# A softmax over 16,384 rows with held stores, growing tiles and a row-maximum step on GpSimd

## The chip, the cores and the metric

The kernel runs on one core of a Trainium2 chip. The metric is the device time of one execution, in microseconds (us). The profile covers the span from the first to the last instruction of one of these executions. On this core four engines matter: VectorE (DVE), ScalarE (ACT), GpSimd (POOL) and SyncE (SP). Sixteen DMA engines move data between the large memory (HBM) and the on-chip memory (SBUF). Each instruction stream that issues transfers feeds a queue of its own on all sixteen of them.

## The reference

The input is 16 x 1024 rows of 512 single-precision numbers. Each row gets a softmax with temperature 2:

```python
x_scaled = x / 2.0
x_max = np.max(x_scaled, axis=-1, keepdims=True)
exp_x = np.exp(x_scaled - x_max)
return exp_x / np.sum(exp_x, axis=-1, keepdims=True)
```

Input and output are 33.55 MB each. A softmax doesn't change when the same number is subtracted from all elements of a row, so the number that is subtracted is a choice within what the exponential can represent.

## The kernel before

Rows are counted here per partition: the 16,384 rows are 128 for each of the 128 partitions, and "a row" below means one row on every partition, 262,144 bytes.

`PLAN` (L11 to L14) lists twelve tiles. A tile is what one load and one store move. Each entry has the tile's chunks, in rows, and the place where the tile begins in the arena, a buffer of 100 rows in SBUF. A chunk is what one step of VectorE and ScalarE treats. There are tiles of 3, 7, seven times 15, and then 7, 3 and 3 rows. The result replaces the input in the same place of the arena. The first eight tiles have places of their own; the last four reuse the places of earlier tiles, and `behind` (L63 to L68) lists whose. Each partition's part of a tile is one contiguous run, 2,048 bytes per row of the tile, so a transfer is 128 runs, eight on each DMA engine.

Per chunk k there are four steps:

- `do_max` (L83): VectorE reduces each row to its negated maximum in `negmax`, once the tile's load has landed.
- `compute_and_store`, L109 to L121: ScalarE computes the exponential of 0.5 times the input plus `negmax`, row by row, in place, and sums each row into `sums`. The shift is the whole maximum, not half of it.
- `do_mul` (L92): VectorE takes the reciprocal of the sums and multiplies each row by it.
- L131 to L141: SP waits for the last multiply of a tile and issues its store.

VectorE's order is written out at L124 to L128: the maximum of chunk k, then the multiplies of chunk k - LAG, with LAG of 2. So it treats the maximum of two later chunks before it needs a chunk's sums.

Loads of the first eight tiles are issued by ScalarE at the beginning, two of them ahead of the program's opening barrier (`issue_loads`, L77). Loads of the last four are issued by SP, on the same queue as the stores, two stores after the store whose place they take and after waits on that store's landing (L135 to L139). At the end SP waits for every store (L140 to L141). Each tile has a semaphore for its load and one for its store, and s_max, s_exp, s_rec and s_mul count chunks through the four steps.

Of the kernel before, what the change touches and what calls it, by code (L numbers as in the profile page):

```python
# [1 line left out]

# [4 lines left out]

PLAN = [  # L11
    ([3], 0), ([4, 3], 3), ([5] * 3, 10), ([5] * 3, 25), ([5] * 3, 40), ([5] * 3, 55),
    ([5] * 3, 70), ([5] * 3, 85), ([5] * 3, 10), ([4, 3], 3), ([3], 0), ([3], 25),
]  # L14
ARENA = 100
LAG = 2


@with_exitstack
def kernel(  # L20
    ctx: ExitStack,
    tc: tile.TileContext,
    x: bass.AP,
    out: bass.AP,
):
    nc = tc.nc
    fp32 = mybir.dt.float32

    xf = x.flatten_outer_dims()
    of = out.flatten_outer_dims()  # L30
    N, D = xf.shape
    P = nc.NUM_PARTITIONS
    n_rows = N // P
    assert sum(sum(c) for c, _ in PLAN) == n_rows

    arena = nc.alloc_sbuf_tensor("arena", (P, ARENA, D), fp32)
    negmax = nc.alloc_sbuf_tensor("negmax", (P, n_rows), fp32)
    sums = nc.alloc_sbuf_tensor("sums", (P, n_rows), fp32)
    recip = nc.alloc_sbuf_tensor("recip", (P, n_rows), fp32)

    tiles, chunks, base = [], [], 0
    for t, (cs, at) in enumerate(PLAN):
        r = sum(cs)
        tiles.append((base, r, at))
        o = 0
        for c in cs:
            chunks.append((t, base + o, c, at + o))
            o += c  # L50
        base += r
    last_chunk = {c[0]: k for k, c in enumerate(chunks)}

    def dram(ap, t):
        b, r, _ = tiles[t]
        return ap[b * P : (b + r) * P].rearrange("(p r) d -> p r d", r=r)

    def sb(t):
        _, r, at = tiles[t]
        return arena[:, at : at + r, :]  # L60


    behind = {}  # L63
    for t, (_, r, at) in enumerate(tiles):
        for u in range(t):
            _, ru, au = tiles[u]
            if at < au + ru and au < at + r:
                behind.setdefault(t, []).append(u)  # L68

    ld = [tc.alloc_semaphore(f"ld{t}") for t in range(len(tiles))]  # L70
    st = [tc.alloc_semaphore(f"st{t}") for t in range(len(tiles))]
    s_max = tc.alloc_semaphore("s_max")
    s_exp = tc.alloc_semaphore("s_exp")
    s_rec = tc.alloc_semaphore("s_rec")
    s_mul = tc.alloc_semaphore("s_mul")

    def issue_loads(begin, end):  # L77

        for t in range(begin, end):
            if t not in behind:  # L80
                nc.scalar.dma_start(out=sb(t), in_=dram(xf, t)).then_inc(ld[t], 16)

    def do_max(k):  # L83
        t, b, c, a = chunks[k]
        nc.vector.reduce_max(  # L85
            out=negmax[:, b : b + c],
            in_=arena[:, a : a + c],
            axis=mybir.AxisListType.X,
            negate=True,
        )._wait_ge(ld[t], 16).then_inc(s_max, 1)  # L90

    def do_mul(k):  # L92
        t, b, c, a = chunks[k]
        nc.vector.reciprocal(  # L94
            out=recip[:, b : b + c], in_=sums[:, b : b + c]
        )._wait_ge(s_exp, k + 1).then_inc(s_rec, 1)
        for r in range(c):
            ins = nc.vector.tensor_scalar_mul(  # L98
                out=arena[:, a + r],
                in0=arena[:, a + r],  # L100
                scalar1=recip[:, b + r : b + r + 1],
            )
            if r == 0:
                ins._wait_ge(s_rec, k + 1)
        ins.then_inc(s_mul, 1)

    def compute_and_store():

        for k, (t, b, c, a) in enumerate(chunks):  # L109
            for r in range(c):  # L110
                ins = nc.scalar.activation(  # L111
                    out=arena[:, a + r],
                    in_=arena[:, a + r],
                    func=mybir.ActivationFunctionType.Exp,
                    bias=negmax[:, b + r : b + r + 1],
                    scale=0.5,
                    accum_out=sums[:, b + r : b + r + 1],
                )
                if r == 0:
                    ins._wait_ge(s_max, k + 1)  # L120
            ins.then_inc(s_exp, 1)  # L121


        for k in range(len(chunks) + LAG):  # L124
            if k < len(chunks):
                do_max(k)
            if k >= LAG:
                do_mul(k - LAG)  # L128


        late = sorted(behind)  # L131
        for t in range(len(tiles)):
            nc.sync.wait_ge(s_mul, last_chunk[t] + 1)
            nc.sync.dma_start(out=dram(of, t), in_=sb(t)).then_inc(st[t], 16)
            while late and max(behind[late[0]]) <= t - 2:  # L135
                u = late.pop(0)
                for v in behind[u]:
                    nc.sync.wait_ge(st[v], 16)
                nc.sync.dma_start(out=sb(u), in_=dram(xf, u)).then_inc(ld[u], 16)  # L139
        for t in range(len(tiles)):  # L140
            nc.sync.wait_ge(st[t], 16)  # L141

    hook = nc.inst_callbacks[-1]
    nc.remove_inst_callback(hook)
    symbolic = nc._always_lower_symbolic_ap
    nc._always_lower_symbolic_ap = False
    here = str(nc.cur_bb)
    entry = nc.main_func.blocks[0]  # L150
    head, jumps = entry.instructions[:-5], entry.instructions[-5:]
    entry.instructions = []
    nc.switch_bb("main", None)
    issue_loads(0, 2)
    first = list(entry.instructions)
    at = next(k for k, i in enumerate(head) if type(i).__name__ == "InstDrain")
    entry.instructions = head[:at] + first + head[at:]
    issue_loads(2, len(tiles))
    compute_and_store()
    entry.instructions = list(entry.instructions) + jumps  # L160
    nc.switch_bb(here, None)
    nc._always_lower_symbolic_ap = symbolic
    nc.push_inst_callback(hook)


# [1 line left out]
_INS = ['x']  # L167
_OUTS = [((16, 1024, 512), 'float32')]


# [23 lines left out]
```

## Time and profile before

| what | value |
|---|---|
| median of four executions | 162.87 us (162.7 to 163.48) |
| the profiled execution | 163.48 us |
| its span | 161.7 us |
| bytes read / written | 33.55 MB / 33.55 MB |
| mean transfer rate over the span | 415 GB/s |
| maximum of a 5-row chunk (DVE) | 2,814 ns, 21 of them |
| multiply of one row (DVE) | 482 ns, 128 of them, one begun every 0.41 us |
| exponential of one row (ACT) | 710 ns, 128 of them, one begun every 0.70 us |
| small set-up fill on GpSimd | 99 to 102 ns, 4 of them |

The profile's page begins with the busy time of each engine as a share of the span. Its second part cuts the span into 40 equal slices, one digit each: 9 means busy for 90% or more. The row called DMA there is the mean over the sixteen DMA engines. A third part has the DMA queues: q10 is ScalarE's, q1 is SP's; the figures are packets, megabytes, and the time the packets took as a share of sixteen engines' span. The chain of waits is followed back from the last instruction to what released it, and so on to the beginning; it doesn't always follow transfers. An instruction's duration includes its start and its drain, and the next of its engine can begin before it ends, so the distance from start to start is what a series costs.

### The profile page before, as it was taken

The page shows a single profiled execution, that of the slowest core. Times are in us where ns is not written, and L with a number is a line of the kernel's source. Part 1 is how long each engine was busy: PE and PEld are TensorE (multiplying, and loading weights), DVE is VectorE, ACT ScalarE, POOL GpSimd, SP SyncE. Part 2 cuts the span into 40 slices and gives each one's busy share as a digit, 9 for nine tenths or more (in the row PEclk, how much of TensorE's full clock was granted, in tenths as well). Part 3 has the DMA queues.
Part 4 walks back from the last instruction along what each step waited for, and adds up shares of the span by engine and source line. Part 5 has one row for each costly group of instructions (what it writes and reads, how often), then busy time and mean ns, then how long its engine had stood idle before and what let it go on. Part 6 is the DMA issues. An engine that isn't in the chain of part 4 may idle for free.

```text
span 161.7 us, 513 instructions
## 1 busy us (share of the span) xinstructions
DVE 126.3 (78%) x184; ACT 94.5 (58%) x257; POOL 0.2 (0%) x4
## 2 busy tenths in 40 slices
DVE  0475599999999999998899839999999999930000
ACT  0739087866688666787378625667976875500000
POOL 0000000000000000000000000000000000000000
DMA  7999999899999999999999899999999999999991
GB/s 275 450 410 456 418 436 438 340 472 394 463 395 458 395 464 403 448 426 433 456 403 471 388 458 403 456 388 420 448 391 465 441 426 441 448 418 433 396 409 76
DMA packets 3460, 67.14 MB, mean 415 GB/s; under 512 B 385, under 2 KB 385, under 8 KB 1153
## 3 DMA queue, kind: packets, MB, share of 16 engines
q1 hardware_dynamic: 2304, 40.90, 59.1%
q10 hardware_dynamic: 1152, 26.21, 38.5%
q14 instruction: 4, 0.02, 0.0%
HBM read 33.55 MB, written 33.55 MB: 415 GB/s over the span
## 4 chain that ended last, share of the span: by engine, by line
DVE 74%; DMA 10%; another core or an unknown queue 3%; issue 0%; DVEq 0%
DVE negmax L85 40%; DVE arena L98 32%; DMA arena<-in_x_dram 10%; DVE recip L94 2%; DVEq L189 0%
## 5 line engine op out<-in xcount | busy, mean ns | idle before, releaser
L111 ACT ACTIVATE arena<-arena,negmax 128x512 f32<-128x512 f32 x128 | 90.7, 710 | 42.0 <-DVE negmax L85 42.0
L85 DVE TENSOR_REDUCE negmax<-arena 128x5 f32<-128x2560 f32 (+2 forms) x28 | 72.3, 2585 | 15.8 <-DMA arena<-in_x_dram 15.8
L98 DVE TENSOR_SCALAR arena<-arena,recip 128x512 f32<-128x512 f32 x128 | 53.2, 482 | 1.0
L111 ACT ACTIVATION_READ_ACCUMULATOR arena<-arena,negmax 128x1 f32 x128 | 23.9, 187 | 0.0
L94 DVE RECIPROCAL recip<-sums 128x5 f32<-128x5 f32 (+2 forms) x28 | 4.9, 176 | 0.0
L111 ACT ACT_TABLE_LOAD x1 | 1.3, 1283 | 4.5 <-issue 4.5
L178 POOL MEMSET const-bfloat16-1.0<- 128x1 bf16 x1 | 0.1, 102 | 0.0
L178 POOL MEMSET const-uint8-127<- 128x1 uint8 x1 | 0.1, 102 | 0.0
L178 POOL MEMSET const-float32-0.0<- 128x1 f32 x1 | 0.1, 99 | 0.2 <-issue 0.2
L178 POOL MEMSET const-float32-1.0<- 128x1 f32 x1 | 0.1, 99 | 0.0
## 6 DMA issues: line engine op xcount, KB each, us to landing
out_dram<-arena SPq DMA_DIRECT2D x7, 3840.0 KB, 26.0
arena<-in_x_dram ACTq DMA_DIRECT2D x6, 3840.0 KB, 48.1
arena<-in_x_dram SPq DMA_DIRECT2D x1, 3840.0 KB, 36.0
out_dram<-arena SPq DMA_DIRECT2D x2, 1792.0 KB, 17.0
out_dram<-arena SPq DMA_DIRECT2D x3, 768.0 KB, 17.1
arena<-in_x_dram ACTq DMA_DIRECT2D x1, 1792.0 KB, 8.4
arena<-in_x_dram SPq DMA_DIRECT2D x1, 1792.0 KB, 39.8
arena<-in_x_dram SPq DMA_DIRECT2D x2, 768.0 KB, 39.7
```

What stands on the lines that cost most here:

```text
L85: nc.vector.reduce_max(out=negmax[:, b : b + c], in_=arena[:, a : a + c], axis=mybir.AxisListType.X, negate=True,)._wait_ge(ld[t], 16).the ...
L94: nc.vector.reciprocal(out=recip[:, b : b + c], in_=sums[:, b : b + c])._wait_ge(s_exp, k + 1).then_inc(s_rec, 1)
L98: ins = nc.vector.tensor_scalar_mul(out=arena[:, a + r], in0=arena[:, a + r], scalar1=recip[:, b + r : b + r + 1],)
L111: ins = nc.scalar.activation(out=arena[:, a + r], in_=arena[:, a + r], func=mybir.ActivationFunctionType.Exp, bias=negmax[:, b + r : b + r ...
L178: nc = _bacc.Bacc("TRN2", target_bir_lowering=False, num_devices=1)
```

## The change

The plan has ten tiles instead of twelve, with rows 3, 5, 9, 15, 21, 21, 21, 15, 11, 7. The first seven have places of their own in the arena (96 of its 100 rows), the last three reuse places. Chunks have up to 7 rows.

Stores are held: no store is issued before chunk `HOLD` (4) has been multiplied. From then on a store follows its tile's last multiply as before.

Late loads move from SP's queue to ScalarE's. ScalarE issues the load of tile 7 after the exponentials of the last chunk of tile 4, and those of tiles 8 and 9 after the last chunk of tile 5 (`AFTER`), each behind waits for the stores whose places they take.

Between the maximum and the exponential there is a new step: GpSimd multiplies the chunk's negated maxima by 0.5 into a new small tensor `bias`, and ScalarE's exponential takes `bias` and waits for that step's semaphore instead of the maximum's. The shift is then half the maximum, as in the reference.

The closing waits for stores are on GpSimd instead of SP, and stores that nobody else waits for share one semaphore.

```diff
 PLAN = [
-    ([3], 0), ([4, 3], 3), ([5] * 3, 10), ([5] * 3, 25), ([5] * 3, 40), ([5] * 3, 55),
-    ([5] * 3, 70), ([5] * 3, 85), ([5] * 3, 10), ([4, 3], 3), ([3], 0), ([3], 25),
+    ([3], 0), ([5], 3), ([5, 4], 8), ([5] * 3, 17), ([7] * 3, 33), ([7] * 3, 54),
+    ([7] * 3, 75), ([5] * 3, 0), ([6, 5], 15), ([4, 3], 26),
 ]
 ARENA = 100
 LAG = 2
+HOLD = 4
+AFTER = {7: 4, 8: 5, 9: 5}
+EARLY = 2
+FIRST = [("scalar", [(0, 128)])]
...
+    bias = nc.alloc_sbuf_tensor("bias", (P, n_rows), fp32)
...
-    def issue_loads(begin, end):
-
-        for t in range(begin, end):
-            if t not in behind:
-                nc.scalar.dma_start(out=sb(t), in_=dram(xf, t)).then_inc(ld[t], 16)
+    def do_load(engine, t, groups=((0, P),)):
+        for u in behind.get(t, []):
+            engine.wait_ge(st[u], 16)
+        for p, q in groups:
+            engine.dma_start(out=sb(t)[p:q], in_=dram(xf, t)[p:q]).then_inc(ld[t], 16)
+
+    def do_early():
+        for name, groups in FIRST:
+            do_load(getattr(nc, name), 0, groups)
+        for t in range(1, EARLY):
+            do_load(nc.scalar, t)
...
+        for t in range(EARLY, len(tiles)):
+            if t not in behind:
+                do_load(nc.scalar, t)
+        late = sorted(behind)
         for k, (t, b, c, a) in enumerate(chunks):
+            while late and last_chunk[AFTER[late[0]]] < k:
+                do_load(nc.scalar, late.pop(0))
             for r in range(c):
                 ins = nc.scalar.activation(
                     out=arena[:, a + r],
                     in_=arena[:, a + r],
                     func=mybir.ActivationFunctionType.Exp,
-                    bias=negmax[:, b + r : b + r + 1],
+                    bias=bias[:, b + r : b + r + 1],
                     scale=0.5,
                     accum_out=sums[:, b + r : b + r + 1],
                 )
                 if r == 0:
-                    ins._wait_ge(s_max, k + 1)
+                    ins._wait_ge(s_bias, k + 1)
             ins.then_inc(s_exp, 1)
+
+        for k, (t, b, c, a) in enumerate(chunks):
+            nc.gpsimd.tensor_scalar_mul(
+                out=bias[:, b : b + c], in0=negmax[:, b : b + c], scalar1=0.5
+            )._wait_ge(s_max, k + 1).then_inc(s_bias, 1)
...
-        late = sorted(behind)
+        ends = 0
         for t in range(len(tiles)):
-            nc.sync.wait_ge(s_mul, last_chunk[t] + 1)
-            nc.sync.dma_start(out=dram(of, t), in_=sb(t)).then_inc(st[t], 16)
-            while late and max(behind[late[0]]) <= t - 2:
-                u = late.pop(0)
-                for v in behind[u]:
-                    nc.sync.wait_ge(st[v], 16)
-                nc.sync.dma_start(out=sb(u), in_=dram(xf, u)).then_inc(ld[u], 16)
-        for t in range(len(tiles)):
-            nc.sync.wait_ge(st[t], 16)
+            nc.sync.wait_ge(s_mul, max(last_chunk[t], HOLD) + 1)
+            ins = nc.sync.dma_start(out=dram(of, t), in_=sb(t))
+            if t in awaited:
+                ins.then_inc(st[t], 16)
+            else:
+                ins.then_inc(s_end, 16)
+                ends += 16
+
+        for t in awaited:
+            nc.gpsimd.wait_ge(st[t], 16)
+        nc.gpsimd.wait_ge(s_end, ends)
```

## The prediction

> **What bounds the kernel now.** I read the page's engine and slice lines first, since they say which resource is never free.
>
> ```profile
> span 161.7 us, 513 instructions
> DVE 126.3 (78%) x184; ACT 94.5 (58%) x257; POOL 0.2 (0%) x4
> ...
> DMA  7999999899999999999999899999999999999991
> ...
> q1 hardware_dynamic: 2304, 40.90, 59.1%
> q10 hardware_dynamic: 1152, 26.21, 38.5%
> ...
> DVE 74%; DMA 10%; another core or an unknown queue 3%; issue 0%; DVEq 0%
> ```
>
> VectorE leads the chain with 74%, but it is idle for 22% of the span, while the two DMA queues (q10 is ScalarE's, the first loads; q1 is SP's, stores and late loads) fill 59.1 + 38.5 = 97.6% of sixteen engines' time. The chain ends at VectorE's last multiply, at 143.0, and doesn't follow the stores behind it. The stretches at the end, asked for by window (columns: DVE, ACT and POOL busy, clock, DMA share, GB/s), show what it omits:
>
> ```profile
> 152.00:156.00 4.00, 0.00 (x0) 0.00 (x0) 0.00 (x0) 1.00 0.97 413
> ...
> 157.00:158.00 1.00, 0.00 (x0) 0.00 (x0) 0.00 (x0) 1.00 0.93 387
> 158.00:159.00 1.00, 0.00 (x0) 0.00 (x0) 0.00 (x0) 1.00 0.33 135
> 159.00:160.00 1.00, 0.00 (x0) 0.00 (x0) 0.00 (x0) 1.00 0.12 49
> 160.00:161.70 1.70, 0.00 (x0) 0.00 (x0) 0.00 (x0) 1.00 0.01 4
> ```
>
> All compute is over by 143, the DMA engines stay full to 158, and then a few of them run on alone to 160.6. Two questions decide: does the DMA stream get shorter, and does the slowest DMA engine fall less far behind?
>
> The packet records of the trace size the stream. Each transfer is 8 packets on each of 16 engines and one semaphore write of 9 ns. A packet took (median) 1138 ns for 30,720 bytes, 535 for 14,336 and 234 for 6,144: 36.8 ns per 1,000 bytes plus 7.5 ns. One engine's work before is 2 x 8 x (7 x 1.138 + 2 x 0.535 + 3 x 0.234) + 24 x 0.009 = 156.0 us. First packet at 1.2, so an engine that loses nothing is done at 157.2. The last store's sixteen semaphore increments came from 158.0 to 160.6: 0.8 of loss and landing for the fastest, 2.6 more for the slowest. Another 1.1 us of closing barrier gives the span, and 1.8 outside it the 163.48 of this execution (the highest of four; median 162.87).
>
> The spread of 2.6 has a history. It was 0.9 to 1.0 at the first three loads, still 1.0 when tile 4's store landed (97.0 to 98.0), 1.8 at the next load, and 2.5 at the small load landing from 112.0 to 114.5. So 1.6 us was lost by slow engines between 98 and 114, when q10 was empty and loads stood alone in q1.
>
> **What the skill says.** "DMA: Bandwidth & Descriptors", Queues, rings and completion order: an engine goes round-robin between queues, draining a packet of typically 9 to 17 descriptors from one before it switches. The trace differs: from 20 to 28 us, with whole loads of 30,720-byte packets against a store of 6,144-byte ones, the queues advance nearly one descriptor for one.
>
> ```profile
> q10 hardware_dynamic: 84, 2.58, 75.0%
> q1 hardware_dynamic: 93, 0.57, 17.0%
> ```
>
> I use one for one below. The same page, Anatomy of one DMA: semaphore waits happen on the issuing sequencer before dispatch; the DMA engines only consume queues. The trace agrees (SP waits 135.5 us for multiplies while queues stay full). So a load that waits on ScalarE's queue stops the exponentials behind it. "SBUF — State Buffer", Who interferes with whom: a tensor_scalar in a two-port mode and a GpSimd operation lock each other out; tensor_reduce doesn't. The trace of before cannot show that, but the multiplies do run in a fast mode: 512 elements per 0.41 us, against 0.55 for the maximum's. "GPSIMD Engine Reference", 3.1, has 769 ns for 512 elements at 1.8 cycles each, so the 3 to 7 elements here are nearly all fixed cost.
>
> **The change, part by part.**
>
> *Transfers.* Twenty instead of 24. Bytes are the same; the work per engine becomes 16 x (0.234 + 0.384 + 0.686 + 2 x 1.138 + 3 x 1.590 + 0.837 + 0.535) + 20 x 0.009 = 155.7, with new sizes from the line above. **-0.3 us**, on the path.
>
> *Held stores.* They cost nothing as long as no engine runs dry. Durations: maximum 0.54 per row, multiply 0.41 per row + 0.13 for the reciprocal, ScalarE 0.70 per row. Loads of tiles 0 to 3 land by about 22; VectorE runs max 0 (done 6.4), max 1 (10.7), max 2 (16.3), mul 0, max 3 (20.0), mul 1, max 4 (25.6), mul 2, max 5, mul 3, max 6, mul 4: done at 37.3. The first store of before went at 14.3, the held ones go at 37.3. Until then q10 has only loads, 95 rows queued, of which tile 5 is under way at 37: engines full. Then one for one: 8 packets of store 0 beside 8 of tiles 5 and 6 (8 x 1.82 us) to 52; 6.5 of store 1 beside the rest (6.5 x 1.97) to 64.7, when all first loads are in; the rest of store 1 and store 2 alone to 70.8, landed by about 72.
>
> *Late loads on ScalarE.* After chunk 9 (about 59) ScalarE must wait for stores 0, 1, 2, so chunk 10's exponentials, ready at 60, start at 72.5: **12 us lost there**, and VectorE waits for them in mul 10 from 73 to 77.5. Behind it, chunks 10 to 12 and the store of tile 5 come late, at 94. The steps of 7-row chunks, 3.8 for a maximum and 2.9 for a multiply: max 7 done 41.1, mul 5 43.3, max 8 47.1, mul 6 49.3 (store 3 goes), max 9 53.1, mul 7 56.0, max 10 59.8, mul 8 62.7, max 11 66.5, mul 9 69.4 (store 4 goes), max 12 73.2, mul 10 80.4, max 13 84.2, mul 11 87.1, max 14 90.9, mul 12 93.8 (store 5 goes).
>
> Are the engines fed meanwhile? In q1, store 3 starts at 70.8; from 72 its last 7 packets alternate with load 7 (2 x 1.138 each) to about 87, then store 4 with the rest of load 7 (2.73 each) and with load 8 (issued after chunk 12's exponentials, at 88; 2.43 each) to about 106. Slack for store 5: 12 us. Onward by the same two rules: store 5 lasts to 124, and store 6 goes at 112; load 9 lands at 129; store 6 lasts to 137, and store 7 goes at 127; store 7 lasts to 146, and store 8 goes at 138; store 8 lasts to 153, and store 9 goes at 141, or at 144 if load 9 lands 2 to 3 us late. Smallest slack 8 to 9 us. The three DMA issues on ScalarE, 0.5 each by the trace, are inside it. So **0**.
>
> *GpSimd.* 23 small multiplies between maximum and exponential. From below, the MEMSET row's 0.10 us; from above, one that waits out seven multiplies, 3 us. Even that doesn't hold mul k: with LAG 2 it comes two maxima and two multiplies after max k (10 us for 5 rows, exponentials 3.5). For VectorE the lock could cost 0.1 to 0.4 each; I take 0.1, 2.3 us in all, inside the slack of 8. **0**; what queues behind a waiting multiply on GpSimd is only the next one, and at the end the closing waits.
>
> *Closing waits* move from SP to GpSimd, which leads the barrier anyway (SP's steps from 160.6 to 160.9). From -0.2 to +0.1; I take **-0.1**.
>
> *Spread.* In the new order late loads have stores beside them in the other queue, where the spread of before did not grow (1.0 at 18, 1.0 at 97). That can return 0 to 1.6; but 22 us more of loads run alone at the beginning. There it didn't grow before either (8 to 18 us), over few microseconds. I take half, **-0.8**.
>
> Sum: 163.48 - 0.3 - 0.1 - 0.8 = **162.3**, which is 0.6 under the median, 0.35%. A difference under 0.3% (0.5 us) can't be told from none here.
>
> **The rivals.**
> - *All of the spread is regained* (chance 0.17): 163.48 - 0.4 - 1.6 = 161.5. For it: 80 us of two-queue traffic without growth. Against it: the median execution lies 0.6 under the profiled one, so part may be missing there already.
> - *Loads alone lose time* (0.22): the slower side. Place: 15 to 37 us, 22 us more with q10 alone. Price: the rate of the 98 to 114 stretch, 1.6 us of lag in some 17 us of loads, so 2.1. With nothing regained elsewhere, 162.87 - 0.4 + 2.1 = 164.6; with half regained 163.8. It decides from 0.9 us of added lag. For it: both bad spots of before are loads in a lone queue; against it: 439 GB/s from 2 to 14 us.
> - *Engines run dry* (0.06): if store 2 lands after 84 instead of 72 (queues not shared one for one), or GpSimd's lock costs VectorE over 0.4 us per chunk (8 to 9 us over 23), every further microsecond is one lost: at 4 us, 166.5.
> - *The sharing or holding does nothing at all* is within the forecast's own upper part: 162.6 from the transfers alone.
>
> **How the numbers follow.** The forecast has 0.55, own range 161.7 to 163.0, of it 0.30 under the bound of 162.4 and 0.25 within. Faster: 0.30 + 0.17 = 0.47; slower: 0.22 + 0.06 = 0.28, with a little of it within; so 0.47, 0.27, 0.26. Leaving out half of the best case's lower side and the drained engines, the range is 161.2 to 164.3.
>
> **What would show it.** Right: no DMA slice under 9 before 156, twenty transfers, first store at about 37, an idle stretch of some 12 us on ScalarE near 60 with VectorE idle after it, engines still full when VectorE ends near 141 to 144, and a last-store spread of 1 to 2 us. Wrong: a slice of low DMA share between 60 and 130, a rate under 425 GB/s in the loads before 37, a spread growing there, or VectorE still busy when the stores run out.

## The result and the profile after

The changed kernel takes 163.47 us (median of 43 executions, 162.35 to 164.78); the kernel before took 162.91 (64 executions, 162.23 to 163.94). The ratio is 1.0043, with a 95% interval of 1.003 to 1.0055: slower by 0.43%, where 0.35% faster had been forecast. The time lies within the widest range that was given (161.2 to 164.3), above the forecast's own (161.7 to 163.0), and on the wrong side of no change. The executions also scatter twice as much as before (standard deviation 0.64 against 0.34 us). Ratios and intervals, here and below, leave out executions in the slow state, over 1.5% above the fastest of their kernel (two of 16 in run 1, one of 6 in run 6), which the medians given there include.

The page of the kernel after, from one execution of 163.40 us:

```profile
span 161.6 us, 522 instructions
...
DVE 125.3 (78%) x174; ACT 93.7 (58%) x257; POOL 5.7 (4%) x27
...
DMA  7999999999999999999999999999998998999991
...
q10 hardware_dynamic: 1440, 33.56, 49.1%
q1 hardware_dynamic: 1440, 33.56, 48.4%
...
DMA 63%; DVE 16%; ACT 9%; ACTq 1%; SPq 0%; issue 0%; DVEq 0%
```

The DMA row is as full as before (49.1 + 48.4 = 97.5%), all loads are now in q10 and all stores in q1. The chain now goes through transfers for 63% of the span. That is no new bound: the same full DMA engines are now also what VectorE's chain hangs on. The waits (who waited for whom, total us, times, longest):

```profile
ACT arena L139 <- POOL bias L153: 30.3, 16, 7.4
DVE negmax L106 <- DMA arena<-in_x_dram: 15.7, 5, 6.6
ACT arena L139 <- DMA out_dram<-arena: 14.4, 1, 14.4
DVE recip L115 <- ACT arena L139: 4.4, 1, 4.4
```

The third line is the late load that waits on ScalarE's queue for store 2, with the exponentials behind it, and the fourth is what VectorE waits for it. Neither reaches the end. That is read from the last microseconds (columns: the stretch, busy time of DVE, ACT and POOL, clock, DMA share, GB/s):

```profile
156.00:157.00 1.00, 0.00 (x0) 0.00 (x0) 0.00 (x0) 1.00 0.97 416
157.00:158.00 1.00, 0.00 (x0) 0.00 (x0) 0.00 (x0) 1.00 0.61 258
158.00:159.00 1.00, 0.00 (x0) 0.00 (x0) 0.00 (x0) 1.00 0.40 172
159.00:160.00 1.00, 0.00 (x0) 0.00 (x0) 0.00 (x0) 1.00 0.14 57
```

A share of 0.40 is some six of sixteen engines, 0.14 some two. From the semaphore increments of the last store: ten engines were done between 157.8 and 158.4, six between 159.4 and 160.6. The fastest was 0.2 us earlier than before (157.85 against 158.06). The last was as late as in the profile of before, 160.6, but that execution, 163.48, was 0.6 above its kernel's median, and this one is at its median. In all twenty profiles of this study the time is the landing on the slowest engine plus 2.8 to 3.2 us, so the medians put the slowest engine near 160.0 before and 160.6 after; that is an estimate, not a reading. What has to be explained is this lag of the slow engines behind the fastest.

### The profile page after: what moved, and what is told of

Same layout as the page of the kernel before. It is cut to its first block, busy times and chain, and to the rows that moved or that the text cites. A ratio compares the mean times of both kernels' runs of the same rounds, so it can differ in the third digit from the quotient of the medians.

```text
span 161.6 us, 522 instructions
## 1 busy us (share of the span) xinstructions
DVE 125.3 (78%) x174; ACT 93.7 (58%) x257; POOL 5.7 (4%) x27
## 3 DMA queue, kind: packets, MB, share of 16 engines
q10 hardware_dynamic: 1440, 33.56, 49.1%
q1 hardware_dynamic: 1440, 33.56, 48.4%
## 4 chain that ended last, share of the span: by engine, by line
DMA 63%; DVE 16%; ACT 9%; ACTq 1%; SPq 0%; issue 0%; DVEq 0%
DMA arena<-in_x_dram 42%; DMA out_dram<-arena 21%; ACT arena L139 9%; DVE arena L119 8%; DVE negmax L106 8%; ACTq L94 1%; SPq L168 0%; DVE recip L115 0%; DVEq L224 0%; ACTq L92 0%
## 5 line engine op out<-in xcount | busy, mean ns | idle before, releaser
L139 ACT ACTIVATE arena<-arena,bias 128x512 f32<-128x512 f32 x128 | 90.6, 709 | 45.7 <-POOL bias L153 30.3
L106 DVE TENSOR_REDUCE negmax<-arena 128x5 f32<-128x2560 f32 (+4 forms) x23 | 71.7, 3116 | 15.7 <-DMA arena<-in_x_dram 15.7
L139 ACT ACTIVATION_READ_ACCUMULATOR arena<-arena,bias 128x1 f32 x128 | 23.9, 187 | 0.0
L153 POOL TENSOR_SCALAR bias<-negmax 128x5 f32<-128x5 f32 (+4 forms) x23 | 5.5, 238 | 135.2 <-DVE negmax L106 135.2
L115 DVE RECIPROCAL recip<-sums 128x5 f32<-128x5 f32 (+4 forms) x23 | 4.2, 182 | 4.4 <-ACT arena L139 4.4
```

The costliest lines, as they stand in the source:

```text
L106: nc.vector.reduce_max(out=negmax[:, b : b + c], in_=arena[:, a : a + c], axis=mybir.AxisListType.X, negate=True,)._wait_ge(ld[t], 16 if t ...
L115: nc.vector.reciprocal(out=recip[:, b : b + c], in_=sums[:, b : b + c])._wait_ge(s_exp, k + 1).then_inc(s_rec, 1)
L139: ins = nc.scalar.activation(out=arena[:, a + r], in_=arena[:, a + r], func=mybir.ActivationFunctionType.Exp, bias=bias[:, b + r : b + r + 1],
L153: nc.gpsimd.tensor_scalar_mul(out=bias[:, b : b + c], in0=negmax[:, b : b + c], scalar1=0.5)._wait_ge(s_max, k + 1).then_inc(s_bias, 1)
```

## The experiments

Each kernel was timed in five rounds beside the kernel before, and profiled once. The runs fell on four chips. The kernel before was timed on each of them, with medians of 162.63 to 162.78 us; no other kernel was timed on two of the four. "Spread" is the time from the first to the last of the sixteen engines in the landing of the last store, in the profiled execution. That execution can lie away from its kernel's median (164.09 against 163.00 in run 7), so a spread belongs to one execution and the ratio to the kernel. A packet is called late where it took over 0.15 us more than the median packet of its size.

**1. The change without the GpSimd step.**

```diff
-                    bias=bias[:, b + r : b + r + 1],
+                    bias=negmax[:, b + r : b + r + 1],
...
-                    ins._wait_ge(s_bias, k + 1)
+                    ins._wait_ge(s_max, k + 1)
```

> The changed kernel without the GpSimd step: ScalarE takes the whole negated maximum and waits for VectorE directly, as before the change. Theory L (the loss is lag of slow DMA engines, made by the transfers' plan): nothing is regained, time stays at 163.2 to 163.7, 0.2 to 0.5% over the kernel before. Rival G (the GpSimd step costs it, by its lock with VectorE or by its end): back to 162.4 to 162.9, and the spread of the last store's landing falls from 2.8 to about 2.

Measured: 164.01 us, ratio 1.0066 (1.0041 to 1.0091), spread 2.6. Nothing was regained, the time is even above theory L's range; GpSimd is not the cause.

**2. The GpSimd step alone, in the kernel before.** The same lines the other way round.

> The kernel before with the GpSimd step alone. Theory L: no difference that can be measured, 162.7 to 163.1. Rival G: 163.2 to 163.7, as the whole change.

Measured: 163.00, ratio 1.0016 (1.0002 to 1.003). Within theory L's range: barely more than nothing, and under the 0.3% called tellable.

**3. The stores not held.**

```diff
-HOLD = 4
+HOLD = 0
```

> The changed kernel with the stores not held (HOLD 0 instead of 4): the first store goes at about 18 instead of 36.8, and store 2 lands before 60, so that ScalarE's stall of 14.4 us shrinks or goes. If the hold makes the loss (loads alone in the first 37 us): 162.5 to 162.9. If the loss is in the large tiles or in the late loads' queue: 163.2 to 163.7.

Measured: 162.75, ratio 0.9999 (0.9981 to 1.0017). The whole loss is gone, but not by the path that the expectation gave. Store 2 landed at 71.4, not before 60, since 43,008-byte load packets pass small store packets one for one. ScalarE's stalls behind stores, 14.6 us in two pieces, are there without the hold too, and cost nothing:

```profile
ACT arena L139 <- DMA out_dram<-arena: 14.6, 2, 12.5
```

Lag isn't gone from its profile either: the spread is 2.1, and twelve packets after 71 us were late, where the change had 18.

**4. The late loads back on SP's queue.**

```diff
-            while late and last_chunk[AFTER[late[0]]] < k:
-                do_load(nc.scalar, late.pop(0))
...
+            while late and AFTER[late[0]] <= t:
+                do_load(nc.sync, late.pop(0))
```

> The changed kernel with the three late loads issued by SP behind stores 4, 5 and 5 instead of by ScalarE. ScalarE's stall of 14.4 us goes. If late loads in a second queue beside stores make slow engines fall behind (their lag grew from 1.1 us at 72 to 2.6 at 105): lag below 2, time 162.5 to 162.9. If the queue is indifferent: 163.2 to 163.7.

Measured: 163.08, ratio 1.0019 (1.0006 to 1.0032), spread 1.7. The time is between the two expectations, the spread is the first one's. About half of the loss is gone, with the hold still in place.

**5. The hold alone, in the kernel before.**

```diff
+HOLD = 5
...
-            nc.sync.wait_ge(s_mul, last_chunk[t] + 1)
+            nc.sync.wait_ge(s_mul, max(last_chunk[t], HOLD) + 1)
```

> The kernel before with nothing but the stores held until chunk 5 has been multiplied (25 rows, first store near 32 us). Theory H (holding by itself makes slow engines fall further behind, whatever the plan): 163.2 to 163.7, last-store spread 2.3 to 2.8. Rival S (only this combination of hold, large tiles and late loads does it): 162.6 to 163.0.

Measured: 163.75, ratio 1.0054 (1.0036 to 1.0073). The time is theory H's, or just above it; the place isn't: the spread is 1.3, and the fastest engine is 0.9 later than before (158.9). The first store went at 41.6, not 32: the expectation had left out VectorE's lag of two chunks.

**6 and 7. The change with HOLD 8, and with HOLD 2.**

> The changed kernel with HOLD 8 instead of 4 (first store near 62 us). Theory H: as slow as the change or slower, 163.5 to 164.2. Rival S: no order in the hold, anything from 162.7 to 163.7. If the engines run dry of stores or loads for some time, it shows as a slice of low DMA share.

> The changed kernel with HOLD 2 (first store near 27 us). Theory H: between HOLD 0 (162.75) and HOLD 4 (163.47), near 163.1. Rival S: no order.

Measured: HOLD 8 166.48, ratio 1.0232 (1.0198 to 1.0266); HOLD 2 163.00, ratio 1.0012 (0.9996 to 1.0028), its one profile, of 164.09, with a spread of 3.4. HOLD 2 fits theory H; HOLD 8 is above every expectation. With HOLD 8 the engines run dry, as these windows of it show:

```profile
56.00:60.00 4.00, 3.96 (x4) 1.94 (x6) 0.24 (x1) 1.00 0.70 301
60.00:62.00 2.00, 2.00 (x6) 0.00 (x0) 0.00 (x0) 1.00 0.00 0
62.00:64.00 2.00, 2.00 (x2) 0.00 (x0) 0.00 (x0) 1.00 0.41 169
64.00:68.00 4.00, 3.96 (x7) 0.00 (x0) 0.24 (x1) 1.00 1.04 430
```

The first loads were all in by 60.7, the first store was issued at 62.4: sixteen engines with nothing to do, and the fastest of them is done at 162.5 instead of 157.8. Its spread is only 0.7. This is a bound on the hold that the change, with a first store at 36.8, is far from.

**8. The change with no tile over 15 rows.**

```diff
-    ([3], 0), ([5], 3), ([5, 4], 8), ([5] * 3, 17), ([7] * 3, 33), ([7] * 3, 54),
-    ([7] * 3, 75), ([5] * 3, 0), ([6, 5], 15), ([4, 3], 26),
+    ([3], 0), ([5], 3), ([5, 4, 3], 8), ([5] * 3, 20), ([5] * 3, 35), ([5] * 3, 50),
+    ([5] * 3, 65), ([5] * 3, 80), ([5] * 3, 0), ([6, 5], 15), ([4, 3], 26),
...
-AFTER = {7: 4, 8: 5, 9: 5}
+AFTER = {8: 5, 9: 6, 10: 6}
```

> The changed kernel with hold and late loads as they are, but no tile over 15 rows (3, 5, 12, five of 15, then 15, 11, 7; late loads behind tiles 5, 6, 6). If packets of 43,008 bytes are needed for the loss: 162.6 to 163.0. If the hold does it alone: 163.2 to 163.7.

Measured: 162.08, ratio 0.996 (0.9946 to 0.9974): faster than both kernels and under both expectations, with the hold in place. So a hold of four chunks doesn't by itself make a kernel slower than the one before.

**9. The same plan without the hold** (HOLD 0).

> The plan without tiles over 15 rows, as in the faster kernel (162.08), with HOLD 0 instead of 4. If the hold costs time in every plan (theory H): it gets faster still, 161.6 to 161.9. If hold and large tiles lose only together (theory HT): no difference, 161.9 to 162.3. If the hold is a gain once the tiles are small: 162.4 to 162.8.

Measured: 169.26, ratio 1.0378 (1.0338 to 1.0418), outside every expectation. Its windows at the end:

```profile
157.00:158.00 1.00, 0.00 (x0) 0.00 (x0) 0.00 (x0) 1.00 0.78 332
158.00:159.00 1.00, 0.00 (x0) 0.00 (x0) 0.00 (x0) 1.00 0.23 96
159.00:160.00 1.00, 0.00 (x0) 0.00 (x0) 0.00 (x0) 1.00 0.10 45
...
162.00:164.00 2.00, 0.00 (x0) 0.00 (x0) 0.00 (x0) 1.00 0.13 57
164.00:166.00 2.00, 0.00 (x0) 0.00 (x0) 0.00 (x0) 1.00 0.10 43
```

A share of 0.10 to 0.13 for six microseconds is two engines of sixteen. The last store landed on fourteen engines from 158.2 to 159.3, on the other two at 166.1 and 166.3. The packet records show how they fell behind: between 71 and 127 us, packets of 30,720 bytes that take 1,138 ns elsewhere come with up to 0.6 us more, nearly all of them in pairs at the same moment. All of them are in q1, the queue of the stores. After 60 us 36 packets were late, 14.3 us together; shared by two engines, that is about 7 us each, most of their lag. Some of these pairs (start in us, queue, bytes, excess in ns):

```
84.50 q1 30720 +610   84.53 q1 30720 +597
87.38 q1 30720 +584   87.39 q1 30720 +586
90.24 q1 30720 +583   90.25 q1 30720 +576
93.09 q1 30720 +566   93.09 q1 30720 +589
```

**10 and 11. The 21-row tiles stored in pieces of 7 rows, or loaded in pieces of 7 rows.**

```diff
+                    nc.sync.dma_start(
+                        out=dram(of, t)[:, 7 * i : 7 * i + 7],
+                        in_=sb(t)[:, 7 * i : 7 * i + 7],
+                    ).then_inc(s_end, 16)
```

> The changed kernel with the three 21-row tiles stored in three pieces of 7 rows each, behind each chunk's multiplies; loads stay whole. If the 43,008-byte packets of the stores are what slow engines lose time on beside loads (their slow packets at 100 to 103 and 119 to 123): 162.2 to 162.8, six more transfers included (0.4 us). If it is the loads' size, or the hold alone: 163.4 to 164.0.

> The changed kernel with the three 21-row tiles loaded in three pieces of 7 rows; stores stay whole. If the large loads matter, since they pass the held stores one packet for one: store 2 lands before 65, ScalarE's stall of 14.4 us shrinks, and the time falls to 162.3 to 162.8. If the stores' size matters: 163.4 to 164.0.

Measured: stores in pieces 162.49, ratio 0.9981 (0.9968 to 0.9993), spread 1.7; loads in pieces 165.37, ratio 1.0162 (1.0128 to 1.0197), spread 4.4. The first is as expected for large store packets; in the profile of the change, store packets of 43,008 bytes at 100 to 103 and 121 to 123 us take 0.2 to 0.85 us over their 1.59, and with pieces there is one slow store packet between 70 and 126, beside eight slow load packets at 87 to 91. But pieces also leave earlier than whole tiles. The second is a poor test, and outside both expectations: the last three of ScalarE's thirteen load issues at the beginning took 2.6, 6.7 and 6.1 us, so that its exponentials began late and the first store went at 44.8.

**12. The faster plan without the GpSimd step.**

> The faster plan without tiles over 15 rows, without the GpSimd step. If GpSimd costs what it seemed to alone (0.16%): 161.8. If it costs nothing: 162.0 to 162.2.

Measured: 162.18, ratio 0.9955 (0.994 to 0.997). GpSimd costs nothing that can be told in this plan either.

**13. The small-tile plan with HOLD 1**: one store of 3 rows goes at 23.6 instead of 19.2 us, nothing else is altered.

> The small-tile plan with HOLD 1: against HOLD 0 only the first store of 3 rows moves, from 19.2 to about 23.6 us. If the time hangs on how stores and loads happen to line up (theory P): away from 169.3 by more than 2 us, 162 to 166. If a short hold is bad in this plan for its length: 168 to 170.

Measured: 162.27, ratio 0.9981 (0.9969 to 0.9992), as theory P allows. That is seven microseconds for a single small store moved by four. Runs 9 and 13 were on two chips, where the kernel before had medians of 162.68 and 162.66. In its profile no packet after 60 us is late by over 0.15, the spread is 1.4, and its windows at the end are:

```profile
157.00:158.00 1.00, 0.00 (x0) 0.00 (x0) 0.00 (x0) 1.00 0.67 287
158.00:159.00 1.00, 0.00 (x0) 0.00 (x0) 0.00 (x0) 1.00 0.14 57
159.00:160.00 1.00, 0.00 (x0) 0.00 (x0) 0.00 (x0) 1.00 0.00 0
```

**14. The plan of run 9 with its late loads on SP.**

> The small-tile plan with HOLD 0, its late loads issued by SP behind stores 5, 6 and 6. If slow engines lose their time on stores beside loads of the other queue (theory Q): the two slow engines stop falling behind when the first loads are in, near 83 us, and the time falls from 169.3 to 162.3 to 164.5. If the two engines are slow for another reason: 168 to 170.

Measured: 165.06, ratio 1.0155 (1.013 to 1.0179). Theory Q, that stores lose only beside loads of the other queue, isn't borne out: slow engines went on falling behind after 83 us, from 97 to 109, with everything in one queue (4.0 us at load 8, at 113). The end is a different loss, though: the loads landed late, a store came too late behind them, and from 138 to 142 the engines had too little to do (DMA share 0.70).

**15 and 16. The change with HOLD 3, and with HOLD 5.**

> The changed kernel with HOLD 3. Theory H (length of the hold): between HOLD 2 (163.0) and HOLD 4 (163.47). Theory P (how stores and loads line up): anything from 162.4 to 164.5, out of order being the telling case.

> The changed kernel with HOLD 5 (first store near 43 us; first loads last to about 65, so nothing runs dry). Length of the hold: 163.5 to 164.5 and not under HOLD 4. Theory P: no order, 162.4 to 164.5; under 163.2 speaks against a price per length.

Measured: HOLD 3 164.33, ratio 1.01 (1.007 to 1.013), spread 3.0; HOLD 5 162.97, ratio 1.0019 (1.0007 to 1.0031), spread 1.9. The series of ratios for HOLD 0, 2, 3, 4, 5 is 0.9999, 1.0012, 1.01, 1.0043, 1.0019: no order. The kernels with HOLD 0, 2, 3 and 5 ran on four different chips, so the comparison rests on the ratio to the kernel before on each.

**17. Run 5 with the three small last tiles made one.**

```diff
-    ([5] * 3, 70), ([5] * 3, 85), ([5] * 3, 10), ([4, 3], 3), ([3], 0), ([3], 25),
+    ([5] * 3, 70), ([5] * 3, 85), ([5] * 3, 10), ([5, 5, 3], 25),
```

> The kernel before with the hold (chunk 5), and its last three tiles of 7, 3 and 3 rows made one of 13. In hold alone all engines lost 0.8 us on the 6,144-byte packets of one 3-row load at 110 us. If those small loads alone in a queue are its cost: 162.4 to 162.8, with the fastest engine done near 158.0 instead of 158.9. If the hold costs it elsewhere: 163.3 to 163.8.

Measured: 163.58, ratio 1.0054 (1.0032 to 1.0076). The fastest engine is back at 157.9, as expected of small loads taken away, but the slowest is at 160.7, against 160.2 in run 5, now from packets of 30,720 bytes that were slow at 95 and 104 us. The time is no better.

**18. The kernel before with its first store alone held**, to 22.7 us.

> The kernel before with its first store alone held, until chunk 1 has been multiplied (from 14.3 to about 22.7 us). Theory P: a shift by more than 0.3% either way is possible, within 162.0 to 164.0. Length of the hold: under 0.1%, 162.6 to 162.9.

Measured: 164.41, ratio 1.0109 (1.0088 to 1.013), beyond even theory P's range. One store of 3 rows, eight microseconds later, costs the kernel before more than the whole change does.

## Why the prediction was wrong

**What held.** Most of the working came out closely. Twenty transfers instead of 24 gave a stream that was 0.2 us shorter on the fastest engine (0.3 forecast). The first store went at 36.8 (37.3 forecast). ScalarE waited 14.4 us for store 2 (12 forecast), chunk 10's exponentials began at 72.3 (72.5), and VectorE waited 4.4 us behind it (4.5). The last store was issued at 146.2 (141 to 144), with the store ahead of it landing on no engine before 153.6, so it had some 7 us of slack (8 to 9). No engine ran dry: by the forecast's own figures its packets alone would have ended at 156.9, and the fastest engine was done 0.9 to 1.0 later, before the change 0.9. (The two slices of 8 in the DMA row, from 121 and from 133 us, each follow a stretch of over 1.0.) The forecast that the engines take one packet from each queue in turn, against the Trainium skill's page "DMA: Bandwidth & Descriptors" (Queues, rings and completion order), carried the schedule of the queues; loads were in at 65.2, where 64.7 was forecast.

The GpSimd term was right too. The operation took 228 to 246 ns. The multiplies took 482 ns on average before:

```profile
L98 DVE TENSOR_SCALAR arena<-arena,recip 128x512 f32<-128x512 f32 x128 | 53.2, 482 | 1.0
```

and after, where the second line is GpSimd's operation:

```profile
L119 DVE TENSOR_SCALAR arena<-arena,recip 128x512 f32<-128x512 f32 x128 | 52.8, 482 | 0.8
L153 POOL TENSOR_SCALAR bias<-negmax 128x5 f32<-128x5 f32 (+4 forms) x23 | 5.5, 238 | 135.2 <-DVE negmax L106 135.2
```

Yet 20 of GpSimd's 23 operations lay beside a multiply (one from 52.61 to 52.85 us, with a multiply begun at 52.67). These multiplies took 485 to 491 ns, as a chunk's first multiply did before (485 to 489). So the lock that the Trainium skill's page "SBUF — State Buffer" (Who interferes with whom) describes cost VectorE nothing visible here, less than the 0.1 us per chunk that I took. The closing barrier took 1.07 us after the last landing instead of 1.09, so the -0.1 for it didn't come.

**The step that failed** is the term called Spread, -0.8, the largest of the sum. It rested on the reading that slow engines don't fall further behind while late loads have stores beside them in the other queue (1.0 at 18 us, 1.0 at 97). In the changed kernel they fell behind just there: the spread was 0.8 at 35 us, with loads alone, 1.1 when store 2 landed at 72, 2.5 when store 4 landed at 107, and 2.7 from 123 us on. So it ended at 2.7, where the sum had 1.8. Counted from the profile of before (2.6 in the forecast, 2.5 by the exact increments), the term was +0.1 to +0.2 instead of -0.8.

The sum also started from that profile's 163.48, 0.6 above its kernel's median, though the forecast noticed this; run 2, with the same transfers, shows a spread of 1.6. Counted from the medians, with an estimated 2.0 before and 2.8 after, the term was +0.8; with -0.2 from the stream that is the +0.6 measured.

The place that the forecast blamed, loads alone in a queue, was not wrong for the kernel before: with its order of late loads the spread grows at that place in runs 17 and 18 too (from 1.3 to 2.8 and from 1.4 to 2.3 between 98 and 115 us). What was wrong is the belief that loads with stores beside them would keep the engines together.

**The rivals.** "Loads alone lose time" named the right side and the right kind of loss, lag of slow engines, in the wrong place, and at 163.8 to 164.6 too dear. "Engines run dry" was not met in the change, but run 6 shows that it is real where the hold is long.

**What the runs settle.** GpSimd is not the cause (runs 1, 2, 12). What the loss is made of can be read from the packets: in the profile of the change 18 packets after 71 us were late, eleven of stores and seven of loads, 7.1 us together. From store 2 to the last store, the sixteen engines' lags behind the fastest, added up, grew by 8.8 us. The two sums are close, so late packets account for most of the lag.

No single part of the change owns this loss. It is gone without the hold (run 3), but with the hold in place it is also gone with smaller tiles (run 8) or with stores in pieces (run 10), and about half of it is gone with the late loads on SP (run 4) or with a longer hold (run 16). Short of running dry, no price of the hold itself can be seen: its series has no order (0.9999 to 1.01), with small tiles 1 and 4 chunks of hold are faster than before while none is 3.8% slower (runs 8, 9, 13), and the kernel before loses 1.1% from one small store moved (run 18).

That the moment of one small store is enough to change the time is shown by runs 13 and 18, which alter nothing else; run 18 has the kernel before on the same chip beside it.

**What they leave open.** That such a moment acts by the way in which stores and loads then line up is argued: the pairs of run 9, late at the same moment, and their absence in run 13 fit it. What makes such a packet slow is not shown: two queues at once aren't needed (run 14), nor are 43,008-byte packets (run 9) or small loads (run 17). The packet records don't say which engine a packet was on, so whether the slow engines are always the same ones can't be told. The store pieces of run 10 fit a share of the large packets in the change itself, without proving it.

## What to carry to other kernels

Where the DMA engines are full from beginning to end, as here, read the last store engine by engine: the time was that of the slowest engine, and the mean share of sixteen didn't show it until the last microseconds. Don't book the lag in a single profile as a loss to be regained; profile the same transfers twice and hold the profiled execution against the median first. And before a small gain or loss is ascribed to an idea such as holding stores, shift one unimportant transfer by a few microseconds: here that alone moved the time by -4% in one plan and +1% in another, more than the idea under test.

## What the runs showed of the hardware that was not expected

- With nothing changed but one small store, two of sixteen DMA engines came to lag 8 us each, through pairs of packets that were late at the same moment by up to 0.6 us (run 9 against run 13, on two chips).
- In the small-load stretch of run 18, at 110 to 113 us, 6,144-byte packets took up to 0.86 us over their usual 0.234, and over forty of them were late by more than 0.15; in the kernel before nine of the same packets were.
- Issuing a transfer isn't always cheap: the eleventh to thirteenth loads issued in a row by ScalarE took 2.6, 6.7 and 6.1 us instead of about 0.5 (run 11), and three load issues of SP from 71.6 us on took 2.1 to 2.2 us (run 18), where the same three took 0.5 to 0.6 in the kernel before. Why isn't shown.
